# Chunk products by row halves in turn, one half's PSUM tile from another pool

## The chip, the cores and the metric

One NeuronCore of a Trainium2 chip runs the whole forward pass. TensorE (PE) multiplies into PSUM, VectorE (DVE), ScalarE (ACT) and GpSimd (POOL) work on tiles in SBUF and PSUM, and SyncE (SP) issues the DMAs. Each engine runs its instructions in the order in which they stand in its stream. The metric is the device time of one execution in microseconds, as the median of several runs; less is better.

## The reference, cut to what matters

Six layers and a final norm, on 256 tokens of width 2048. The first and the fourth are RWKV-7 mixers: five kinds of projections, and per head (32 heads of 64) a recurrence over tokens.

```
xx = shift(h) - h
r, k, v, g = [(h + xx * mu[j]) @ w_in[j] for j in range(4)]
...
def step(state, inp):                        # per head, S is 64 x 64
    r_t, w_t, k_t, v_t, a_t, b_t = inp
    sa = einsum('bhij,bhj->bhi', state, a_t)
    state = state * w_t + sa * b_t^T + v_t * k_t^T
    y_t = einsum('bhij,bhj->bhi', state, r_t)
...
y = group_norm(y) + bonus
return (y * silu(g)) @ w_out
```

The other layers are attention, pooling, an LRU with attention, and an mLSTM; the change does not touch their code.

## The kernel before

**Projections.** `proj` (line 239) makes one 256 x 512 output: 96 matmuls of line 262, three for each product, since an f32 operand is split into a high and a low part (`wh`, `wl`, `ah`, `al`; lines 220 and 221 split the weights on ACT and DVE). An RWKV layer has k, r and v (two groups of 512 columns each, then again two), then four gate projections, then the output projection, first with chunks 0 to 2 of its input, then with chunk 3. That is 1536 matmuls of line 262 up to the last gate.

**Blocks.** Beside the projections run eight head blocks (`rwkv_block`, four heads of 64 each, 256 columns). Tokens are cut into four chunks of 64, and a block goes through these steps:

- loads, small projections (line 724) and transposes (789), from which `AR` and `BK` come (DVE and POOL, 801 to 815); the bonus (828);
- the chunk products (842): for each half `f` of the block, four chunks `c` and two row halves `hp` of 64 rows, `BK` times `AR` into a PSUM tile for each `hp`, which DVE masks into `GM` (845). Each matmul leaves two records in the trace;
- the elimination: ACT copies (860) and 15 steps on DVE (871 to 881) that end in `Xc`, and from it `X` (932);
- `AV` (904), transposes `BT` (913), and the inversion: two products (929), two of blocks (956) with copies (958, 959) that complete `X`;
- four chunk rounds, each with PE products 990, 998, 1008 and 1022 and copies between them (the output goes to `yt`, 1026);
- group norm (1036 to 1049) and the gate: tile `z` (1055 or 1057). `acts_from` transposes `z` (line 277) and splits it for the output projection.

**PSUM pools.** In an RWKV layer there are four pools of two buffers: `ps` for projections, `gy` for the chunk rounds, `tp` and `gm` for the rest. `tp` serves lines 277, 724, 789, 828 and 842; `gm` serves 904, 913, 929 and 956.

```
BANKS = {True: {"ps": 2, "tp": 2, "gm": 2, "gy": 2}, False: {"ps": 4, "tp": 2, "gm": 2}}
```

Tiles of a pool are handed out in the order in which the program's text asks for them, each as soon as a buffer is free.

**Order.** The text is written by generators that are interleaved by an estimate of PE time (`spawn`, `pump`); blocks start a fixed period apart, and have a high priority (`urgent`). The final order on each engine is made by a scheduler, which orders instructions by priority and by its own timeline, under the data and buffer dependences. So a small edit can move instructions all through a layer.

Of the kernel before, what the change touches and what calls it, by code (L numbers as in the profile page):

```python
# [23 lines left out]
ORDER = mybir.DependencyInfo(mybir.DependencyClass.NoSync, mybir.DependencyReason.DATA)  # L24
# [90 lines left out]
class Builder:  # L115
# [562 lines left out]
    def rwkv_block(self, ia, b):  # L678

        nc, I, S = self.nc, self.I, self.S  # L680
# [89 lines left out]
        AR = self.t("q4", [128, 2, 4, 128], F32, 8)  # L770
        BK = self.t("q4", [128, 2, 4, 128], F32, 8)
# [54 lines left out]
        for t in range(2):  # L826
            for f in range(2):
                nc.tensor.matmul(qb[:, t * 4 + f * 2:t * 4 + f * 2 + 2], pr[:, f, t * 128:t * 128 + 128], rkc[:, f],
                                 start=True, stop=True)
# [5 lines left out]
        GM = self.t("GM", [128, 4, 4, 128], F32, 3)  # L835
        gmask = self.c("gmask")
        for f in range(2):
            qs = [self.p("tp", (128, 4, 128)) for _ in range(2)]
            for c in range(4):
                for hp in range(2):  # L840
                    rs = slice(hp * 64, hp * 64 + 64)
                    nc.tensor.matmul(qs[hp][:, c], BK[rs, f, c], AR[rs, f, c], start=True, stop=True)  # L842
            self.pe(0.9)
            for hp in range(2):
                nc.vector.tensor_tensor(GM[:, f * 2 + hp].rearrange("p (q a) n -> p q (a n)", a=2),  # L845
                                        qs[hp].rearrange("p (q a) n -> p q (a n)", a=2),
                                        gmask[:, f * 128:f * 128 + 256].unsqueeze(1).to_broadcast([128, 2, 256]), OP.mult)
            yield 1.0
# [7 lines left out]
        for i in range(4):  # L856
            rs = slice(i * 32, i * 32 + 32)
# [115 lines left out]
        rows = self.bcast(I["a_rows"][ia, b, 256:768], "rows", 512, 1)  # L973
# [3 lines left out]
        for c in range(4):  # L977
# [18 lines left out]
            for hp in range(2):  # L996
                for f in range(2):
                    nc.tensor.matmul(gy[ar[f], 4 + hp], X[ar[f], (f * 2 + hp) * 2 + pq], G[ar[f], f, hp],
                                     start=first, stop=True, skip_group_check=True)
# [5 lines left out]
            if c < 3:  # L1005
                for hh in range(4):
                    f, hp = hh // 2, hh % 2
                    nc.tensor.matmul(gy[half[hp], 6 + f], BT[:, f * 3 + c, half[hp]], UV[:, hh * 64:hh * 64 + 64],
                                     start=first, stop=True, skip_group_check=True)
# [10 lines left out]
            for hh in range(4):  # L1020
                f, hp = hh // 2, hh % 2
                nc.tensor.matmul(gy[kr[f], hh], GM[:, hh, c, to[f]:to[f] + 64], UV[:, hh * 64:hh * 64 + 64],
                                 start=first, stop=True, skip_group_check=True)
# [838 lines left out]
```

## Time and profile before

| | us |
|---|---|
| median of 3 runs | 3160.73 |
| lowest and highest | 3151.62, 3163.76 |
| the profiled execution | 3169.43 |
| its span | 3167.6 |
| PE busy | 3017.3 (95%) |
| DVE busy | 2247.9 (71%) |
| ACT busy | 1703.7 (54%) |

The span is the time from the first to the last instruction of the profiled execution. Busy time is the union of an engine's instructions; PE is the matmul side, weight loads count apart. A row of a timeline merges equal instructions that follow each other.

### The profile page before, as it was taken

The numbers are of one execution on the slowest core, as the hardware profiler recorded it, in microseconds if no ns is written. First come the engines' busy times: TensorE is split into PE (matmuls) and PEld (weight loads), VectorE is DVE, ScalarE is ACT, GpSimd is POOL, SyncE is SP. The second block draws the span as 40 slices with busy tenths as digits, with TensorE's granted clock in tenths as the row PEclk, the third lists the DMA queues.
The fourth block names the chain that finished last, engine by engine and source line by source line (L and its number), as shares of the span: only waits on it lengthen the run. The fifth ranks groups of instructions, "written<-read, shape, count | busy, mean of one in ns | idle before, by whom it ended". The sixth has DMA issues, their size and how long they took to land. (4 is left out here: it accounts for less than half of the span.)

```text
span 3167.6 us, 48383 instructions
## 1 busy us (share of the span) xinstructions
PE 3017.3 (95%) x17064; PEld 2448.3 (77%) x17064; DVE 2247.9 (71%) x4811; ACT 1703.7 (54%) x3320; POOL 483.3 (15%) x386
## 2 busy tenths in 40 slices
PE   6989999998999999999989899999999999999998
PEld 5777777777888888888867677777777788888886
DVE  7868778765667667676596787898557765756765
ACT  4555555545555555555545554545357755554554
POOL 1012223120112111010011132321201200000101
PEclk9999999998999999999999998999999999999999
DMA  7865564375556556667678555633765566665665
GB/s 235 321 209 169 176 212 148 127 232 184 178 170 179 176 173 215 192 215 214 207 263 280 200 189 175 199 121 121 246 186 157 170 186 193 182 204 169 189 185 169
DMA packets 327011, 610.77 MB, mean 193 GB/s; under 512 B 33856, under 2 KB 60776, under 8 KB 326768
## 3 DMA queue, kind: packets, MB, share of 16 engines
q1 hardware_dynamic: 326768, 607.68, 61.2%
q8 instruction: 134, 2.20, 0.3%
q14 instruction: 109, 0.89, 0.1%
HBM read 544.66 MB, written 62.93 MB: 192 GB/s over the span
## 5 line engine op out<-in xcount | busy, mean ns | idle before, releaser
L221 DVE TENSOR_TENSOR wl<-wr,wh 128x512 fp32r<-128x512 f32 x1728 | 1243.8, 731 | 713.2 <-ACT wh L220 687.3
L220 ACT CAST wh<-wr 128x512 fp32r<-128x512 f32 x1728 | 1055.6, 621 | 1078.3 <-PE qps L262 515.6
L262 PE MATMUL qps<-wl,ah 128*128 128x512 f32 x3424 | 1382.2, 404 | 7.3 <-DVE wl L221 7.2
L262 PE MATMUL qps<-wh,al 128*128 128x512 f32 x3424 | 1364.9, 399 | 2.0 <-DVE al L221 2.0
L262 PE MATMUL qps<-wh,ah 128*128 128x512 f32 x3424 | 1259.0, 404 | 46.1 <-ACT wh L220 11.8
L262 PEld LDWEIGHTS qps<-wh,ah 128*128 128x128 f32 x3424 | 655.1, 192 | 191.6 <-issue 20.4
L262 PEld LDWEIGHTS qps<-wl,ah 128*128 128x128 f32 x3424 | 657.6, 192 | 147.2 <-DVE wl L221 13.1
L262 PEld LDWEIGHTS qps<-wh,al 128*128 128x128 f32 x3424 | 656.0, 192 | 139.9 <-DVE al L221 4.5
L1107 POOL TENSOR_TENSOR q<-q,gain 128x1024 f32<-128x1024 f32 (+1 forms) x15 | 35.0, 2332 | 380.1 <-ACT sq L1101 380.1
L277 PE MATMUL qtp<-cst,q 128*128 128x128 f32 x388 | 62.4, 291 | 30.3 <-DVE q L436 9.7
L482 DVE SCALAR_TENSOR_TENSOR e<-q,vec,q 128x256 f32<-128x256 f32 x192 | 86.6, 504 | 0.0
L277 PEld LDWEIGHTS qtp<-cst,q 128*128 128x128 f32 x388 | 48.8, 149 | 43.7 <-issue 20.5
L842 PE MATMUL qtp<-q,q 64*128 64x128 f32 x512 | 76.3, 312 | 3.5 <-POOL q L815 3.3
L860 ACT COPY Md<-GM 32x128 f32<-32x128 f32 x128 | 54.8, 428 | 38.6 <-DVE GM L845 37.4
L842 PEld LDWEIGHTS qtp<-q,q 64*128 64x128 f32 x512 | 62.7, 209 | 14.6 <-issue 5.9
L1038 POOL TENSOR_TENSOR yt<-yt,gn_m 128x512 f32<-128x512 f32 x16 | 19.1, 1192 | 300.5 <-DVE gn_m L1037 191.6
L321 POOL TENSOR_TENSOR rstd<-rs_v,mhalf 128x2 f32<-128x2 f32 x7 | 5.0, 710 | 383.8 <-DVE rs_v L319 333.6
L304 POOL TENSOR_TENSOR rk_y<-ss,mhalf 128x8 f32<-128x8 f32 x16 | 28.1, 1756 | 217.7 <-DVE ss L715 117.3
L876 DVE TENSOR_TENSOR mb<-mb,Xc 128x120 f32<-128x120 f32 (+14 forms) x240 | 59.8, 249 | 0.4
L845 DVE TENSOR_TENSOR GM<-qtp,cst 128x512 f32<-128x512 f32 x64 | 43.0, 684 | 18.7 <-PE qtp L842 16.7
L871 DVE STREAM_SHUFFLE mb<-Mc 128x120 f32<-128x120 f32 (+14 forms) x240 | 50.6, 223 | 0.1
L881 DVE TENSOR_TENSOR Xc<-Xc,mb 128x112 f32<-128x112 f32 (+6 forms) x224 | 47.6, 213 | 0.1
(377 smaller groups left out, 3032.6 us busy)
## 6 DMA issues: line engine op xcount, KB each, us to landing
wr<-a_w_in SPq DMA_DIRECT2D x256, 512.0 KB
wr<-b_w_in SPq DMA_DIRECT2D x160, 512.0 KB
wr<-odd_w_in SPq DMA_DIRECT2D x128, 512.0 KB
wr<-even_w_in SPq DMA_DIRECT2D x72, 512.0 KB
wr<-a_w_out SPq DMA_DIRECT2D x64, 512.0 KB
wr<-c_w_in SPq DMA_DIRECT2D x64, 512.0 KB
ah<-mix SPq DMA_DIRECT2D x32, 512.0 KB
al<-mix SPq DMA_DIRECT2D x32, 512.0 KB
```

The source lines that it names most:

```text
L220: self.nc.scalar.copy(hi, src)
L221: (eng or self.nc.vector).tensor_tensor(lo, src, hi.bitcast(F32), OP.subtract)
L262: nc.tensor.matmul(o[:, cs], u[:, kk, sl], v[k][:, cs], start=st and x == 0 and c1 == 0, stop=sp and x == 2, skip_group_check=True)
L277: nc.tensor.transpose(q[:, f, t * 128:t * 128 + 128], src[:, t, (fp * 2 + f) * 128:(fp * 2 + f) * 128 + 128], self.ident)
L482: ins = nc.vector.scalar_tensor_tensor(m[:, f], st.xx[c][:, ft], mu, st.h[c][:, ft], OP.mult, OP.add)
L842: nc.tensor.matmul(qs[hp][:, c], BK[rs, f, c], AR[rs, f, c], start=True, stop=True)
L845: nc.vector.tensor_tensor(GM[:, f * 2 + hp].rearrange("p (q a) n -> p q (a n)", a=2), qs[hp].rearrange("p (q a) n -> p q (a n)", a=2), gma ...
L860: nc.scalar.copy(Md[rs, :, us].rearrange("p c u -> p u c"), GM2[rs, us, (1 - i // 2) ^ f, rs])
L871: nc.vector.stream_shuffle(mb[:, 0:15 - r], Mc[:, r + 1:16], [r] * 16 + [r + 16] * 16)
L876: nc.vector.tensor_tensor(mb[:, 0:n], mb[:, 0:n], Xc[:, r:r + 1].to_broadcast([128, n, 8]), OP.mult)
L881: nc.vector.tensor_tensor(Xc[:, r + 2:16], Xc[:, r + 2:16], mb[:, 1:n], OP.add)
L1107: nc.gpsimd.tensor_tensor(e3, e3, gain.unsqueeze(1).to_broadcast([128, 2 * nh, 128]), OP.mult)
```

## The change

For each half `f`, the tile of the second row half comes from `gm` in place of `tp`, and each matmul gets an ordering edge to the one before it, so that the scheduler must keep the order hp 0, hp 1, hp 0, and so on. The edge is one of order on PE and no semaphore.

```
-            qs = [self.p("tp", (128, 4, 128)) for _ in range(2)]
+            qs = [self.p("tp", (128, 4, 128)), self.gm((128, 4, 128))]
+            turn = None
             for c in range(4):
                 for hp in range(2):
                     rs = slice(hp * 64, hp * 64 + 64)
-                    nc.tensor.matmul(qs[hp][:, c], BK[rs, f, c], AR[rs, f, c], start=True, stop=True)
+                    mm = nc.tensor.matmul(qs[hp][:, c], BK[rs, f, c], AR[rs, f, c], start=True, stop=True)
+                    if turn is not None:
+                        self.tc.add_manual_dep(mm.ins, turn.ins.name, ORDER, reason="the halves of the rows take turns")
+                    turn = mm
```

Later lines of the file move down by four; line 842 becomes 843.

First place, the products of block 1 in the first layer, on PE. `qtp` and `qgm` are tiles of the pools `tp` and `gm`, `qps` of a projection; numbers tell tiles apart. Before, around the second row half of f = 0:

```order
L262 MATMUL qps_1514<-wh_1683,al_1253 128x512
L262 MATMUL qps_1513<-wh_1687,ah_1252 128x512
L842 MATMUL qtp_2543<-q4_2409,q4_2410 128x128 x4
L929 MATMUL qgm_2068<-Y_2066,GM_1804 64x64 x16
L842 MATMUL qtp_2560<-q4_2409,q4_2410 128x128 x4
L262 MATMUL qps_1513<-wl_1688,ah_1252 128x512
```

After, the first matmul of f = 0, and the rest of f = 0, which stands 77 projection matmuls further on, behind the last inversion product of block 0:

```order
L917 MATMUL qgm_2037<-cst_96,q4_1708 128x128 x3
L828 MATMUL qtp_2534<-rkc_2495,e2_2452 128x2 x4
L843 MATMUL qtp_2542<-q4_2409,q4_2410 128x128
L262 MATMUL qps_1513<-wl_1666,ah_1181 128x512
L262 MATMUL qps_1513<-wh_1665,al_1182 128x512
```

```order
L960 MATMUL qgm_2158<-X_2061,W_2132 32x32 x15
L843 MATMUL qgm_2543<-q4_2409,q4_2410 128x128
L843 MATMUL qtp_2542<-q4_2409,q4_2410 128x128
L843 MATMUL qgm_2543<-q4_2409,q4_2410 128x128
L843 MATMUL qtp_2542<-q4_2409,q4_2410 128x128
L843 MATMUL qgm_2543<-q4_2409,q4_2410 128x128
L843 MATMUL qtp_2542<-q4_2409,q4_2410 128x128
L843 MATMUL qgm_2543<-q4_2409,q4_2410 128x128
L262 MATMUL qps_1909<-wl_2045,ah_1697 128x512
```

The products of block 1 stood ahead of the inversion's second product before, and stand behind its fourth now. 28 of the 32 halves are cut in this way.

Second place, PE at the end of the gate projections of the first layer, from the last gate matmul on (`qps_6504`). Before, up to the first matmuls of the output projection (`qps_7052`):

```order
L262 MATMUL qps_6504<-wh_6978,al_4810 128x512
L1022 MATMUL qgy_6671<-uv_6672,GM_6068 64x64 x4
L1008 MATMUL qgy_7124<-uv_7125,q4_6911 64x64 x4
L277 MATMUL qtp_7093<-cst_96,z_5468 128x128 x2
L277 MATMUL qtp_7100<-cst_96,z_2572 128x128 x4
L1022 MATMUL qgy_7124<-uv_7125,GM_6714 64x64 x4
L990 MATMUL qgy_7168<-S_7154,q4_6581 128x128 x2
L262 MATMUL qps_7052<-wh_7136,ah_7073 128x512
```

After, the first rows and, further on, those at the first transposes of z:

```order
L262 MATMUL qps_6504<-wh_6978,al_4810 128x512
L1002 MATMUL qgy_5955<-G_5961,X_5656 64x64 x4
L843 MATMUL qtp_6740<-q4_6581,q4_6582 128x128
L933 MATMUL qgm_6306<-Y_6304,GM_6068 64x64 x16
L1012 MATMUL qgy_5955<-uv_5956,q4_5618 64x64 x4
L933 MATMUL qgm_6341<-X_6302,W_6323 64x64 x16
L1026 MATMUL qgy_5955<-uv_5956,GM_5437 64x64 x4
L994 MATMUL qgy_6025<-S_5865,q4_5308 128x128 x2
L960 MATMUL qgm_6380<-Y_6377,GM_6068 32x32 x16
L1002 MATMUL qgy_6025<-G_6031,X_5656 64x64 x4
L960 MATMUL qgm_6415<-X_6302,W_6379 32x32 x16
L843 MATMUL qgm_6716<-q4_6581,q4_6582 128x128
```

```order
L843 MATMUL qgm_6741<-q4_6581,q4_6582 128x128
L843 MATMUL qtp_6740<-q4_6581,q4_6582 128x128
L843 MATMUL qgm_6741<-q4_6581,q4_6582 128x128
L277 MATMUL qtp_7075<-cst_96,z_2572 128x128 x4
L908 MATMUL qgm_6915<-vt_6367,GM_6714 64x64
L1012 MATMUL qgy_6493<-uv_6494,q4_6264 64x64 x4
```

The inversion of block 6 and the products of block 7 stood beside gate matmuls before, and stand between the last gate matmul and the first output matmul now. In the second RWKV layer more stands there: from the inversion of block 5 on.

Third place, PE at the transposes of block 7's output (`qtp_7402`) in the first layer. Before, within the output projection of chunks 0 to 2 (`qps_7675`, `qps_7676`):

```order
L262 MATMUL qps_7676<-wl_7724,ah_7082 128x512
L262 MATMUL qps_7676<-wh_7723,al_7083 128x512
L277 MATMUL qtp_7402<-cst_96,z_6861 128x128 x4
L262 MATMUL qps_7675<-wh_7727,ah_7082 128x512
L262 MATMUL qps_7676<-wh_7727,ah_7082 128x512
```

After, within that of chunk 3 (`qps_7820`, `qps_7821`):

```order
L262 MATMUL qps_7821<-wl_7829,ah_7371 128x512
L262 MATMUL qps_7821<-wh_7828,al_7372 128x512
L1026 MATMUL qgy_7264<-uv_7265,GM_6714 64x64 x4
L277 MATMUL qtp_7402<-cst_96,z_6861 128x128 x4
L262 MATMUL qps_7820<-wh_7846,ah_7371 128x512
```

The transposes stood 54 projection matmuls earlier, and stand directly behind block 7's last chunk product now.

## Rows read from the trace of the kernel before

**Rows 1.** The page, busy time, share and count of each engine:
```profile
PE 3017.3 (95%) x17064; PEld 2448.3 (77%) x17064; DVE 2247.9 (71%) x4811; ACT 1703.7 (54%) x3320; POOL 483.3 (15%) x386
```

**Rows 2.** Windows, blocks' stretches: length, busy by engine, clock, DMA share, GB/s:
```profile
157.05:629.31 472.26, 449.24 (x3642) 355.62 (x3640) 366.47 (x1164) 254.27 (x564) 111.53 (x97) 0.95 0.54 176
1740.49:2208.62 468.13, 437.12 (x3583) 345.50 (x3581) 381.25 (x1174) 246.16 (x549) 115.06 (x97) 0.93 0.52 170
```

**Rows 3.** PE's waits, 157 to 629 us: total us, times, longest:
```profile
PE qgm L913 <- ACT q L915: 4.0, 2, 3.4
```

**Rows 4.** Timeline of PE around the first output matmul: start, us, what:
```profile
626.16 0.39 PE L262 MATMUL qps<-wh,al 128*128 128x512 f32 x1
...
629.31 0.50 PE L262 MATMUL qps<-wh,ah 128*128 128x512 f32 x1
...
2206.70 0.50 PE L262 MATMUL qps<-wh,al 128*128 128x512 f32 x1
...
2208.62 0.50 PE L262 MATMUL qps<-wh,ah 128*128 128x512 f32 x1
```

**Rows 5.** Groups by form, the chunk products: busy us, mean ns, idle before:
```profile
L842 PE MATMUL qtp<-q,q 64*128 64x128 f32 x512 | 76.3, 312 | 3.5 <-POOL q L815 3.3 <-ACT bon L832 0.2
```

**Rows 6.** Timeline of PE, two halves of block 0:
```profile
155.96 1.16 PE L842 MATMUL qtp<-q,q 64*128 64x128 f32 x16
...
161.36 1.71 PE L842 MATMUL qtp<-q,q 64*128 64x128 f32 x16
```

**Rows 7.** Timeline of PE, bursts of one row half, and a lone matmul:
```profile
208.08 1.16 PE L842 MATMUL qtp<-q,q 64*128 64x128 f32 x8
...
521.96 2.07 PE L842 MATMUL qtp<-q,q 64*128 64x128 f32 x8
...
491.92 0.48 PE L842 MATMUL qtp<-q,q 64*128 64x128 f32 x2
```

**Rows 8.** Windows of line 262 alone, first stretch:
```profile
157.05:629.31 472.26, 299.70 (x1132) 215.85 (x1132) 0.95 0.54 176
```

**Rows 9.** Timeline of DVE, block 7 of the first layer: mask, X, last copy:
```profile
554.45 0.69 DVE L845 TENSOR_TENSOR GM<-qtp,cst 128x512 f32<-128x512 f32 x1
...
578.03 1.12 DVE L932 TENSOR_TENSOR X<-Xc,cst 128x512 f32<-128x512 f32 x1
...
605.65 0.42 DVE L959 COPY X<-qgm 32x256 f32<-32x256 f32 x1 [0.24 <-ACT X L958]
```

**Rows 10.** Timeline of DVE: block 0, a chunk round and a mask of the second layer:
```profile
162.56 1.29 DVE L845 TENSOR_TENSOR GM<-qtp,cst 128x512 f32<-128x512 f32 x2 [2.08 <-PE qtp L842]
...
235.74 0.42 DVE L959 COPY X<-qgm 32x256 f32<-32x256 f32 x1
...
1853.11 0.29 DVE L1026 COPY yt<-qgy 64x128 f32<-64x128 f32 x1 [1.13 <-ACT yt L1026]
...
1861.04 0.28 DVE L1026 COPY yt<-qgy 64x128 f32<-64x128 f32 x1
...
2094.02 0.69 DVE L845 TENSOR_TENSOR GM<-qtp,cst 128x512 f32<-128x512 f32 x1 [0.64 <-PE qtp L842]
...
2113.46 1.12 DVE L932 TENSOR_TENSOR X<-Xc,cst 128x512 f32<-128x512 f32 x1
```

**Rows 11.** Timeline, block 7 of the first layer: chunk copies, z, transposes:
```profile
631.82 0.29 DVE L1026 COPY yt<-qgy 64x128 f32<-64x128 f32 x1
...
647.70 0.28 DVE L1026 COPY yt<-qgy 64x128 f32<-64x128 f32 x1
...
677.16 0.28 DVE L1026 COPY yt<-qgy 64x128 f32<-64x128 f32 x1
...
692.19 0.69 DVE L1055 SCALAR_TENSOR_TENSOR z<-yt,z 128x512 f32<-128x512 f32 x1 [1.19 <-POOL yt L1049]
...
696.86 0.60 PE L277 MATMUL qtp<-cst,z 128*128 128x128 f32 x4
```

**Rows 12.** Windows, a stretch with waits in it:
```profile
200.00:250.00 50.00, 44.97 (x353) 36.54 (x354) 35.12 (x123) 23.73 (x50) 10.19 (x10) 0.86 0.57 192
```

## Prediction

> **What bounds the kernel now.** I read the engines' busy shares first: TensorE (PE) is busy 95% of the span [rows 1], nearly all of it with the projections of line 262. So the time changes in two ways only: through PE's own work, and through time in which PE's in-order stream has nothing to run. The change touches the two RWKV layers alone. I cut out of each the stretch in which the eight head blocks run beside the projections [rows 2]: PE is busy 449.2 of 472.3 us and 437.1 of 468.1 us. That leaves 54 us idle in all, in short waits such as the 4.0 us of [rows 3]. The block chain is thus almost wholly hidden, and the question is whether it stays so.
>
> At the end of the gate projections little waits: from the last gate matmul to the first of the output projection PE needs 3.15 us in the first layer (626.16 to 629.31) and 1.9 us in the second [rows 4].
>
> **The chunk products themselves.** The 256 matmuls leave 512 records and 76.3 us of PE [rows 5], 2.38 us for each of 32 halves f (two layers, eight blocks, two halves). The row halves of PE overlap where they alternate: 16 records that do took 1.16 us, 16 that mostly don't 1.71 us [rows 6]. A burst of one row half takes 1.16 us for 8 records, so 2.3 us for both; at a low clock it took 2.07 us [rows 7]. In the order of instructions 7 of the 32 halves alternate wholly before.
>
> After the change 4 of 32 stand in one piece, at 1.16 us. The other 28 are cut as the first place of the order shows: one matmul alone, and 7 alternating much later. A lone matmul takes 0.48 us [rows 7], the seven 7/8 of 1.16, together 1.5 us. That is 4 x 1.16 + 28 x 1.5 = 47 us, 30 us less than 76. Some of the 76 us is low clock, which would strike other instructions instead, so I take **-25 us**, with 0 (the overlap is lost) and -35 as ends. The Trainium skill (TensorEngine Tiling (Array Packing), "Theoretical Speedup") gives up to 2x for a contraction of at most 64 rows; by it the term would be -38 us. The rows with their cut halves give less, and they decide.
>
> **What the second pool costs.** The `gm` tile of a half is asked for after all `gm` tiles of the block before, down to the last of its inversion. The order shows the result: the first product of block 1 goes out early into `tp`, and its `gm` partner stands behind the last inversion product (line 956, 960 after) of block 0. Before, nothing tied them. So the blocks now form one ring: products, mask, elimination, X, four inversion products, next block's products. Meanwhile both `tp` buffers are held by half-made tiles, and what asks for `tp` later waits too, above all the transposes of the gated output (line 277, tile z) that the output projection needs. That is the new wait; I cost it by place.
>
> *Inside a layer* it is covered. Between two blocks' products the order has 167 to 183 projection matmuls in the first four rings of the first layer, at 299.7 us / 1132 = 0.265 us each [rows 8], and some 172 other matmuls of two records. All other PE work of the stretch is (449.2 - 299.7) us over 3642 - 1132 records [rows 2, 8], 60 ns a record. A ring so has 44 + 21 = 65 us of PE work to hide in. The ring itself took 51.6 us in block 7 (554.45 to 606.07) [rows 9] and 73.6 us in block 0 (162.56 to 236.16) [rows 10], both beside a second chain. I take 0, with -15 and +40 as ends.
>
> *End of the gates, first layer.* After the change 150 matmuls stand between the last gate and the first output matmul (20 before): the inversion of block 6, then the products of block 7, then the transposes. 150 x 2 x 60 ns = 18 us is work that merely moved. The gap is longer: from X to the last copy block 7 took 28 us (578.03 to 606.07) [rows 9] between projections, while the vector steps in it sum to some 4 us. Without projections in between I take 14 us, 2.5 us for the products, and 8 us, a fast chunk round (1853.11 to 1861.04) [rows 10], for the round, transposes and split behind them: 24.5 us, **+6 us** over the moved work (0 to 25).
>
> *End of the gates, second layer.* The order has 315 matmuls there (16 before): the inversion of block 5, the products of block 6, its elimination and inversion, the products of block 7. A whole ring is bare. 14 + 2.5 us; then the longer of two chains, mask to X (2094.02 to 2114.58, 20.6 us) [rows 10] and three chunk rounds of block 5 (8 us fast; 15.9 us from 631.82 to 647.70 [rows 11]), for which I take 27 us; then 14 + 2.5 + 8 us: 68 us. 315 x 2 x 60 ns = 38 us of it moved here. **+30 us** (8 to 70).
>
> *End of block 7, both layers.* The blocks end later, and at the third place of the order the last chunk product (line 1022, 1026 after) stands directly ahead of the transposes of block 7's output, behind which only matmuls that need them are left. Before, this had cover: last chunk copy at 677.16, z ready at 692.88, transposes at 696.86 [rows 11], PE running all along. After, it is bare: 15.7 us, and some 1.5 us until the split tiles are there, 17 us a layer: **+34 us** (26 to 42).
>
> *Clock.* The stretch from 200 to 250 us, with short waits in it, ran at a mean granted clock of 0.86 [rows 12] and so lost 7 us of its 50. I take 2 us for each of four long new waits: **+8 us** (0 to 15). The Trainium skill (TensorE: Matmul & The Clock Gate, "HAM oscillation") says that idle gaps put PE back to half rate; the row fits that without proving it.
>
> Vector, scalar and pool work stay the same: the mask reads a PSUM tile of the same size from either pool. Loads keep their bytes; some of later blocks move behind weight loads in SP's queue, and a DMA share of 0.54 and 0.52 [rows 2] leaves room for that, so 0.
>
> Sum: -25 + 0 + 6 + 30 + 34 + 8 = **+53 us**. The profiled execution took 3169.4 us (span 3167.6), 8.7 us above the median of 3160.7; it would become 3222, and against the median **3214 us**, 1.7% slower. A measurement of this kernel tells no less than about 0.5%, 16 us, from no change.
>
> **Rivals.** (a) *Not slower: one ring instead of two chains takes out the idle time inside the layers.* Some of those 54 us [rows 2] come from chains that meet in PE's order, as the wait of the transposes of line 913 for scalar copies [rows 3]. If 37 us or more of the 54 go, the change is within 0.5%; all gone gives 3160. Against it: most are waits inside one chain, and these stay. To be faster by 16 us the bare places must take their short ends besides. 9% within, 3% faster.
> (b) *The ring is longer than its cover.* If it needs 5 us more than its 65 us in each of 14 rings, 70 us come on top: 3284. The 73.6 us of block 0 speaks for it; against it, two chains then shared the vector engine, and one does now. 14%.
> (c) *The products gain nothing*, since pairs into different pools don't overlap or the lone matmul costs more: -25 falls away, 3239. The alternating rows [rows 6] speak against it. 6%.
> My forecast holds 68%.
>
> **Range.** 3168 to 3275: down into the within-0.5% case, up to most of (b); the wide ends of the three bare places make it no narrower. Faster 3%, within 0.5% 9%, slower 88%.
>
> **What will show it.** Products of line 843 (842 before) near 47 us busy. In both layers the mask and scalar copies of a block come only after the inversion's last copies (line 963 after) of the block before. Between the last gate matmul and the output projection a gap of about 25 us in the first layer and 68 us in the second, and some 17 us with PE idle ahead of block 7's transposes in both. If the gaps are 18 and 38 us with PE busy throughout, those terms are mis-sized; if PE idles inside the layers far beyond 54 us, (b) holds; if the blocks' rings still overlap, I have misread the pool.

## The result, and the profile after

The changed kernel takes 3196.15 us (median of 4 runs, 3192.70 to 3199.95), the one before beside it 3162.06: a ratio of 1.0116, 95% interval [1.0098, 1.0133], slower by 1.2%. The profiled executions differ by 29.7 us in span (3197.3, 3167.6). Single executions of one kernel spread: among those of the one before that were run beside run 8 the shortest took 3147.36 us at a granted clock of 0.978 and the longest 3171.49 us at 0.971, so a term of a few us in the balances below is within the scatter.

The page of the changed kernel, to set against [rows 1]: PE is busy 6 us less, and the span is 30 us longer.

```profile
PE 3010.9 (94%) x17064; PEld 2431.1 (76%) x17064; DVE 2239.1 (70%) x4811; ACT 1703.3 (53%) x3320; POOL 476.8 (15%) x386
```

Windows of the chunk products alone, line 843, whole span (length, PE busy, weight loads, clock, DMA share, GB/s). They take 55.9 us where they took 76.3 [rows 5]:

```profile
0.00:3197.30 3197.30, 55.88 (x512) 43.86 (x512) 0.97 0.61 191
```

Where the blocks now meet is seen on DVE at the end of block 0, in the timeline after. Both masks of block 1 (line 849) come only after the last copy of block 0's inversion (line 963), as the one ring has it. The same order holds for every later block in both layers: four masks, then the inversion's last copy, then the next four masks.

```profile
226.89 0.42 DVE L963 COPY X<-qgm 32x256 f32<-32x256 f32 x1 [0.95 <-ACT X L962]
...
228.78 0.69 DVE L849 TENSOR_TENSOR GM<-qtp,cst 128x512 f32<-128x512 f32 x1
229.39 0.68 DVE L849 TENSOR_TENSOR GM<-qgm,cst 128x512 f32<-128x512 f32 x1
```

The windows after, by stage (columns as in [rows 2]). First the blocks' stretch up to the last gate matmul and the gap from there to the first output matmul, in the first and in the second layer:

```profile
162.06:586.01 423.95, 403.19 (x3113) 315.81 (x3112) 333.26 (x1027) 233.24 (x509) 99.80 (x89) 0.97 0.58 190
586.01:614.89 28.88, 23.64 (x284) 19.28 (x282) 21.25 (x53) 14.31 (x39) 9.34 (x8) 0.65 0.15 49
...
1751.34:2150.60 399.26, 375.56 (x2753) 292.66 (x2753) 308.47 (x921) 214.82 (x459) 91.67 (x77) 0.97 0.59 193
2150.60:2218.70 68.10, 53.52 (x595) 42.81 (x594) 48.65 (x172) 29.17 (x78) 20.00 (x18) 0.62 0.13 38
```

The gaps are 28.9 and 68.1 us long (3.15 and 1.9 before [rows 4]), and PE is busy for 82% and 79% of them, at a granted clock of 0.65 and 0.62: it works on the blocks' small products, and no projection runs.

For a balance I cut each layer at the same projection matmuls in both kernels: from block 0's first products to the matmul that stands ahead of block 7's transposes after the change, the wait there, and the rest of the output projection. (Before, these transposes stand 54 projection matmuls ahead of that cut, so there is no wait at it.) Before:

```profile
157.05:710.88 553.83, 526.61 (x4029) 416.97 (x4028) 420.37 (x1252) 289.93 (x630) 129.87 (x109) 0.96 0.56 182
...
711.11:744.72 33.61, 26.19 (x118) 20.77 (x116) 21.01 (x41) 19.84 (x46) 0.71 (x1) 0.87 0.72 230
1740.49:2296.29 555.80, 517.57 (x3983) 409.00 (x3981) 435.63 (x1265) 283.24 (x619) 133.95 (x109) 0.94 0.55 179
...
2296.51:2328.67 32.16, 25.50 (x117) 20.21 (x116) 21.00 (x41) 19.76 (x46) 0.71 (x1) 0.92 0.73 228
```

After:

```profile
162.06:710.30 548.24, 516.88 (x4002) 404.72 (x4000) 416.56 (x1242) 287.11 (x626) 120.80 (x104) 0.96 0.56 183
710.30:725.18 14.88, 1.89 (x14) 1.04 (x13) 4.72 (x10) 2.50 (x5) 6.48 (x5) 0.65 0.41 129
725.18:754.51 29.33, 25.38 (x117) 19.83 (x117) 20.05 (x38) 18.59 (x44) 0.71 (x1) 0.95 0.63 197
1751.34:2313.69 562.35, 519.17 (x3954) 405.08 (x3953) 419.84 (x1257) 283.26 (x617) 123.09 (x103) 0.93 0.53 173
2313.69:2329.25 15.56, 1.89 (x14) 1.04 (x13) 4.79 (x10) 2.51 (x5) 6.48 (x5) 0.67 0.70 221
2329.25:2358.63 29.38, 25.53 (x116) 19.91 (x117) 20.04 (x38) 18.56 (x44) 0.71 (x1) 0.94 0.65 201
```

The first parts change by -5.6 and +6.6 us, the gaps inside them included. Ahead of block 7's transposes there are now 14.9 and 15.6 us (0.2 before), and the rest is 4.3 and 2.8 us shorter. A layer so costs +4.8 and +19.1 us; the remaining 5.8 of the 29.7 us lie outside these stretches.

The bare wait itself in the timeline after. It is the chain of block 7's group norm and gate, where before it ran beside projections [rows 11]:

```profile
710.61 0.46 PE L1026 MATMUL qgy<-uv,GM 128*64 128x64 f32 x8
...
712.10 0.28 DVE L1030 COPY yt<-qgy 64x128 f32<-64x128 f32 x1
...
722.64 0.69 DVE L1059 SCALAR_TENSOR_TENSOR z<-yt,z 128x512 f32<-128x512 f32 x1 [4.11 <-POOL yt L1053]
...
723.39 1.12 PE L277 MATMUL qtp<-cst,z 128*128 128x128 f32 x4 [12.32 <-DVE z L1059]
```

### The profile page after: what moved, and what is told of

Its sections match the earlier page's. It is cut to its first block, busy times and chain, and to the rows that moved or that the text cites. A ratio compares the mean times of both kernels' runs of the same rounds, so it can differ in the third digit from the quotient of the medians.

```text
span 3197.3 us, 48385 instructions
## 1 busy us (share of the span) xinstructions
PE 3010.9 (94%) x17064; PEld 2431.1 (76%) x17064; DVE 2239.1 (70%) x4811; ACT 1703.3 (53%) x3320; POOL 476.8 (15%) x386
## 5 line engine op out<-in xcount | busy, mean ns | idle before, releaser
L262 PEld LDWEIGHTS qps<-wl,ah 128*128 128x128 f32 x3424 | 652.8, 191 | 147.1 <-DVE wl L221 15.6
L277 PEld LDWEIGHTS qtp<-cst,q 128*128 128x128 f32 x388 | 48.1, 147 | 43.3 <-issue 18.5
L801 POOL TENSOR_TENSOR q<-e,e 128x256 f32<-128x256 f32 x32 | 27.8, 889 | 222.5 <-DVE e L799 189.7
L277 PE MATMUL qtp<-cst,z 128*128 128x128 f32 x160 | 28.4, 298 | 27.2 <-DVE z L1059 25.3
L843 PE MATMUL qtp<-q,q 64*128 64x128 f32 x256 | 48.3, 317 | 3.0 <-POOL q L815 3.0
L875 DVE STREAM_SHUFFLE mb<-Mc 128x120 f32<-128x120 f32 (+14 forms) x240 | 50.6, 222 | 0.0
```

What stands on the lines that cost most here:

```text
L262: nc.tensor.matmul(o[:, cs], u[:, kk, sl], v[k][:, cs], start=st and x == 0 and c1 == 0, stop=sp and x == 2, skip_group_check=True)
L277: nc.tensor.transpose(q[:, f, t * 128:t * 128 + 128], src[:, t, (fp * 2 + f) * 128:(fp * 2 + f) * 128 + 128], self.ident)
L843: mm = nc.tensor.matmul(qs[hp][:, c], BK[rs, f, c], AR[rs, f, c], start=True, stop=True)
L875: nc.vector.stream_shuffle(mb[:, 0:15 - r], Mc[:, r + 1:16], [r] * 16 + [r + 16] * 16)
```

## The experiments

Each ratio is to the kernel before, run on the same chip in the same job. The first four were made on the theory that the ring through `gm` is the price, and that it is paid at the layers' ends.

**Run 1, turns without the second pool.**

```
-            qs = [self.p("tp", (128, 4, 128)), self.gm((128, 4, 128))]
+            qs = [self.p("tp", (128, 4, 128)) for _ in range(2)]
```

> Both tiles from tp as before, the ordering edges kept. My theory (the ring through the gm pool costs, the taking of turns gains): no bare places, products near 45 us of PE in place of 76, time 3140 us (3125 to 3160), faster than before. Rival (the edges themselves hold the products of a block back, the pool is harmless): slower than before, 3180 us or more.

Measured: 3180.91 us, 1.0065 [1.0048, 1.0081]. The products took 52.6 us and PE's busy time fell by 20 us, to 2996.8, but the span grew to 3179.3: the saved time came back as idle time. The rival's number came. Turns alone cost time.

**Run 2, the second pool without the turns.**

```
-                    if turn is not None:
-                        self.tc.add_manual_dep(mm.ins, turn.ins.name, ORDER, reason="the halves of the rows take turns")
```

> Second tile from gm, no ordering edges. My theory: the ring stays for the second row half and the products alternate less, so slower than before, 3165 to 3195 us, with the bare wait of some 13 us ahead of block 7's transposes again. Rival (the edges do the harm): 3162 us, as before.

Measured: 3191.73 us, 1.0105 [1.0084, 1.0125]. That is inside the theory's range, and the bare waits ahead of block 7's transposes stand (18.8 and 20.5 us). The pool alone costs nearly as much as the whole change, and so the two costs don't add.

**Run 3, the pools swapped.**

```
-            qs = [self.p("tp", (128, 4, 128)), self.gm((128, 4, 128))]
+            qs = [self.gm((128, 4, 128)), self.p("tp", (128, 4, 128))]
```

> Changed kernel with the pools swapped: the first matmul of a half waits for gm, so no half is cut and no tp buffer is held by a half-made tile. My theory (the ring costs): the bare places stay, 3175 to 3195 us, a little under the changed kernel by the uncut halves (28 x 0.3 = 8 us). Rival (the tp buffers held meanwhile cost): back to 3165 us or less.

Measured: 3203.75 us, 1.0142 [1.0121, 1.0163]. That is above the theory's range. No half waits half made any more, and the products take 40.4 us, the least of all runs; it is the slowest kernel all the same, with 34.3 and 58.4 us at the ends of the gates and 14.9 us ahead of block 7's transposes in both layers. That the held `tp` tiles are the price falls with it.

**Run 4, the last three blocks with both tiles from `tp`.**

```
-            qs = [self.p("tp", (128, 4, 128)), self.gm((128, 4, 128))]
+            qs = [self.p("tp", (128, 4, 128)), self.gm((128, 4, 128)) if b < 5 else self.p("tp", (128, 4, 128))]
```

> Changed kernel, but blocks 5 to 7 of each layer take both tiles from tp. My theory (the cost lies in the bare places at the layers' ends alone, inside a layer the ring is covered): the gaps of 29 and 68 us behind the last gate matmul shrink to 5 us or less, and time falls to 3145 us (3130 to 3165). Rival (the ring also costs inside the layers): 3175 us or more, for five of eight blocks keep it.

Measured: 3189.10 us, 1.0092 [1.0073, 1.0112]. The gaps at the gates' ends fell to 5.3 and 6.7 us, as wanted, and the time hardly followed: the rival's number came, and the bare waits are still there, 16.0 us in each layer. That the gaps in themselves are the price falls too. The next runs cut by blocks, and by what the edges hold.

**Run 5, both tiles from `tp`, and the edges hold one row half after the other.**

```
-            for c in range(4):
-                for hp in range(2):
+            for hp in range(2):
+                for c in range(4):
```

> Edges and tiles as in the run with both tiles from the first pool, but the order that the edges hold is all four products of one row half, then all four of the other: nothing alternates, while both tiles must still be free before the second half starts. The price of alternation alone is the difference to that run. My theory (PE time saved by alternation is real, some 20 us, but the edges that hold a half together delay the blocks and turn it into idle time): the products of line 843 near 74 us busy, block 7 no later than before (its products stand at projection matmuls 1267 to 1308, before 1248 to 1320), idle time near that of before, 3160 to 3170 us. Rival (holding a half together costs some 35 us by itself, whatever the order): 3190 to 3205 us. Rival (the lone order matters for nothing, 3181 as with turns).

Measured: 3144.55 us, 0.9951 [0.9939, 0.9964], below the range expected. The products are back at 72.5 us, and the kernel is 36 us faster than with turns (run 1) and 0.5% faster than before. Windows of the whole span, run 1 and then run 5 (columns as in [rows 2]):

```profile
0.00:3179.30 3179.30, 2996.79 (x17064) 2419.94 (x17064) 2265.83 (x4811) 1704.74 (x3322) 473.01 (x386) 0.97 0.61 192
```

```profile
0.00:3144.00 3144.00, 2999.41 (x17064) 2433.37 (x17064) 2245.75 (x4811) 1703.83 (x3320) 475.85 (x386) 0.98 0.61 194
```

PE is equally busy; run 1 has 182.5 us without PE work, run 5 has 144.6 (before 150.4). A first half that takes turns needs its second tile from its second matmul on; in one piece it goes ahead as soon as its own tile is free. In the order block 7's products end at projection matmul 1384 with turns and 1308 without.

**Runs 6 to 8, by blocks.** Run 6: turns with both tiles from `tp`, in blocks 0 to 4 alone. Run 7: the change in blocks 0 to 4, blocks 5 to 7 as before. Run 8: the reverse of run 7.

```
 run 6   qs = [self.p("tp", (128, 4, 128)) for _ in range(2)]
         if turn is not None and b < 5:
 run 7   qs = [self.p("tp", (128, 4, 128)), self.gm((128, 4, 128)) if b < 5 else self.p("tp", (128, 4, 128))]
         if turn is not None and b < 5:
 run 8   the same two lines with b > 4
```

> Both tiles from the first pool; blocks 0 to 4 alternate by edges, blocks 5 to 7 have no edges, as before. Block 7's products stand at projection matmuls 1304 to 1344 (with edges everywhere 1330 to 1384). My theory (what costs is the late end of the last block's chain): the wait ahead of block 7's transposes in the second layer goes, some 12 us of PE are saved, idle time in the layers stays at some 70 us; 3160 to 3170 us. Rival (waits inside the layers, from chains that meet in PE's order, cost the most): 3175 to 3185 us, as with edges everywhere.

> Blocks 0 to 4 as in the change (second tile from the small pool, edges), blocks 5 to 7 as before. The order has 22 and 20 matmuls at the two ends of the gates (before 20 and 16, the change 150 and 315) and block 7's products at 1418 to 1460. My theory (the ring of the first five blocks moves the whole chain back, and the bare wait ahead of block 7's transposes is what remains of it): the gaps at the end of the gates near 4 us, the bare waits shorter than the change's 15 us a layer, some 5 to 10 us; 3170 to 3180 us. Rival (the ring itself costs inside the layers, the ends nothing): 3185 to 3200 us, as with the last blocks changed in other ways.

> Blocks 5 to 7 as in the change (second tile from the small pool, edges), blocks 0 to 4 as before. The reverse of the run with the change in blocks 0 to 4 alone (3158 us). The order has 15 matmuls at each end of the gates and 12 between the last chunk product and block 7's transposes. My theory now (what costs is what happens to the last three blocks, whatever goes ahead of them): 3180 to 3195 us, with a bare wait of 14 to 18 us ahead of block 7's transposes in both layers. Rival (the price needs the whole ring from block 0 on, and the two halves of it are each free): 3155 to 3170 us.

Measured: run 6 3164.09 us, 1.0017 [1.0004, 1.0030]; run 7 3158.16, 0.9990 [0.9979, 1.0001]; run 8 3188.76, 1.0092 [1.0075, 1.0110]. Run 6 lies in its theory's range, though PE idles for 84 us in its two first parts (65 before). In the time the ring of the first five blocks is free; the change in the last three alone carries most of the price. Run 7 lies below both its ranges, though its bare waits did not shrink to 5 to 10 us as my theory had it. The windows of run 7, cut as above:

```profile
159.64:697.59 537.95, 512.28 (x3993) 401.72 (x3992) 422.47 (x1240) 287.86 (x625) 123.42 (x104) 0.97 0.57 187
697.59:713.64 16.05, 2.35 (x23) 1.35 (x21) 5.01 (x11) 2.68 (x6) 6.48 (x5) 0.69 0.30 104
713.64:742.99 29.35, 25.62 (x116) 19.99 (x117) 20.04 (x38) 18.61 (x44) 0.71 (x1) 0.94 0.63 197
1733.81:2271.16 537.35, 507.09 (x3986) 397.38 (x3984) 425.18 (x1258) 283.25 (x618) 126.25 (x104) 0.97 0.55 182
2271.16:2286.05 14.89, 1.89 (x15) 1.04 (x13) 4.72 (x10) 2.51 (x5) 6.49 (x5) 0.70 0.67 209
2286.05:2315.77 29.72, 26.28 (x116) 20.74 (x117) 20.51 (x40) 18.60 (x44) 0.71 (x1) 0.90 0.63 198
```

The first parts are 15.9 and 18.5 us shorter than before, and pay for the bare waits of 16.1 and 14.9 us. In run 4 the same parts, with the last three blocks taking turns, give most of that back; its windows:

```profile
160.63:713.33 552.70, 512.58 (x3994) 401.59 (x3992) 424.58 (x1240) 287.20 (x625) 119.17 (x104) 0.96 0.56 181
...
1749.23:2302.98 553.75, 515.78 (x3977) 402.71 (x3976) 426.77 (x1259) 282.94 (x617) 126.78 (x106) 0.94 0.54 177
```

552.7 and 553.8 us against 538.0 and 537.4: 31 us, of which PE's busy time is 9 and idle time 22. PE's waits in the first layer's part tell which (total us, times, longest), run 4 and then run 7:

```profile
PE qgm L933 <- DVE Y L942: 5.8, 3, 3.8
PE qgy L1026 <- DVE S L1022: 5.3, 3, 2.9
PE qgy L1026 <- DVE S L1020: 5.1, 2, 3.1
```

```profile
PE qgy L1026 <- DVE S L1020: 3.2, 1, 3.2
...
PE qgy L1026 <- DVE S L1022: 1.0, 2, 0.5
```

The first of these waits does not occur in run 7's part. The long gap of the change has become short waits of the inversion and of the chunk rounds: the wait has moved, and not gone. That holds for the first layer, with 14 of the 22 us. In the second layer the largest difference is another: PE waits 14.1 us for loads at the small projections (line 724), where run 7 waits 7.9.

**Run 9, the change with one row half after the other.** The loops over `c` and `hp` swapped as in run 5, the tiles as in the change.

```
-            for c in range(4):
-                for hp in range(2):
+            for hp in range(2):
+                for c in range(4):
```

> The change with its order turned off: first half into tp, second half into gm, and the edges hold all four products of the first row half ahead of all four of the second, in all blocks. A first half so no longer keeps a tp tile half made while it waits for gm: in the order block 2's first product (projection matmul 592) stands ahead of block 1's last (606), and the gates' ends hold 12 and 19 matmuls (the change 150 and 315). Theory 1 (it is the alternation across two pools, which holds a tp tile until gm comes, that costs): near the pool alone or better, 3160 to 3180 us. Theory 2 (the order of the gm requests alone delays the blocks, as the run with the pool and no edges suggests): 3185 to 3200 us, with a bare wait of some 15 to 20 us ahead of block 7's transposes.

Measured: 3187.44 us, 1.0077 [1.0058, 1.0096]. Theory 2: with the ring loosened and nothing alternating, the requests to `gm` still cost 25 us, and the bare waits stand (14.9 and 17.5 us). Together with the runs before, this tells the pool from the order. The second pool takes the ratio from 1 to 1.0105 without edges (run 2), from 1.0065 to 1.0116 with turns (run 1, the change), and from 0.9951 to 1.0077 with one half after the other (runs 5 and 9): it costs 0.5% to 1.3% in each order. Turns in place of one half after the other cost 1.1% with one pool and 0.4% with two.

**Runs 10 and 11, one row half after the other in the last three blocks,** with blocks 0 to 4 as in run 7 (run 10) and as in run 6 (run 11). Both replace the two loops; tiles of blocks 0 to 4 as there, the others from `tp`.

```
+            for i in range(8):
+                for hp, c in [(i % 2, i // 2) if b < 5 else (i // 4, i % 4)]:
```

> Blocks 0 to 4 as in the change; blocks 5 to 7 with both tiles from the first pool and the edges that hold one row half after the other. If the last three blocks set the price and this order is good for them: 3140 to 3155 us, the bare wait ahead of block 7's transposes at 10 to 16 us. If the 0.5% that the run with one half after the other won was luck of the order: as with blocks 5 to 7 of before, 3155 to 3165 us.

> Both tiles from the first pool; blocks 0 to 4 take turns by edges, blocks 5 to 7 have one row half after the other. Theory (the turns save some 12 us of PE in the first five blocks, the other order keeps the last three early): 3135 to 3150 us, below both kernels. Rival (turns in the first five blocks lose in waits inside the layers what they save, as the run without edges in the last three had it): 3155 to 3170 us.

Measured: 3167.42 us, 1.0018 [1.0005, 1.0030], and 3156.60 us, 0.9984 [0.9967, 1.0001]. Against runs 7 and 6 the same edit is worth, by the ratios, +9 and -10 us. So an edit to the order of three blocks moves this kernel by some 10 us either way without a reason that I could name; run 10 lies above both its ranges, run 11 in its rival's.

**Run 12, the change in blocks 0 to 3 alone.** As run 7 with `b < 4`.

```
             qs = [self.p("tp", (128, 4, 128)), self.gm((128, 4, 128)) if b < 4 else self.p("tp", (128, 4, 128))]
             if turn is not None and b < 4:
```

> Blocks 0 to 3 as in the change, blocks 4 to 7 as before: one block fewer than in the run at 3158 us. In the order block 7's products stand at projection matmuls 1344 to 1392 (there 1418 to 1460), and nothing of the last chunk round stands bare ahead of block 7's transposes in either layer. Theory (each bare wait there costs the kernel 11 to 12 us: some 15 us long, 3 to 4 us given back behind it): 3158 us less 23 us, and 2 to 4 us more for the block that no longer alternates: 3132 to 3145 us. Rival (a bare wait only collects work that must be done anyhow): 3155 to 3165 us.

Measured: 3143.20 us, 0.9951 [0.9934, 0.9968], inside the theory's range, and with run 5 the fastest. But my expectation was wrong in one point: the bare wait went in the first layer only. Windows of run 12:

```profile
157.97:703.71 545.74, 515.46 (x4014) 406.36 (x4013) 428.43 (x1251) 289.44 (x629) 127.88 (x109) 0.97 0.57 185
703.71:703.94 0.23, 0.23 (x3) 0.18 (x1) 0.00 (x0) 0.04 (x1) 0.00 (x0) 1.00 1.00 383
703.94:732.51 28.57, 24.22 (x118) 19.01 (x116) 21.02 (x41) 19.94 (x46) 0.71 (x1) 0.98 0.80 253
1723.83:2255.78 531.95, 505.23 (x3985) 397.12 (x3984) 422.85 (x1260) 283.40 (x618) 129.67 (x106) 0.97 0.56 184
2255.78:2270.67 14.89, 1.89 (x14) 1.04 (x13) 4.72 (x10) 2.51 (x5) 6.49 (x5) 0.66 0.67 211
```

In the first layer the wait (16.1 us in run 7) is gone, the part ahead of it is 7.8 us longer, the rest 0.8 shorter: in this one comparison, in which block 4's products change as well, a bare wait of 16 us is worth 9. In the second layer the wait stays and the part ahead is 5.4 us shorter, so not all of the 12 us between runs 7 and 12 (by the ratios) is the wait's.

**All runs by where block 7's products end** (its last product, counted in projection matmuls from the start, in the order of instructions, in both layers; the last gate matmul is number 1536 in the first layer and 6816 in the second):

| kernel | ends at | products, us | ratio |
|---|---|---|---|
| run 5 | 1308, 6624 | 72.5 | 0.9951 |
| before | 1320, 6624 | 76.3 | 1 |
| run 11 | 1330, 6662 | 59.7 | 0.9984 |
| run 6 | 1344, 6660 | 60.1 | 1.0017 |
| run 1 | 1384, 6699 | 52.6 | 1.0065 |
| run 12 | 1392, 6750 | 63.4 | 0.9951 |
| run 7 | 1460, 6770 | 60.4 | 0.9990 |
| run 10 | 1460, 6779 | 61.7 | 1.0018 |
| run 9 | 1494, 6816 | 71.7 | 1.0077 |
| run 8 | 1513, 6793 | 67.5 | 1.0092 |
| run 4 | 1516, 6796 | 50.6 | 1.0092 |
| run 2 | 1536, 6831 | 70.7 | 1.0105 |
| the change | 1536, 6816 | 55.9 | 1.0116 |
| run 3 | 1536, 6816 | 40.4 | 1.0142 |

Every kernel whose last block comes later than 1460 is slower by 0.8% to 1.4%, whatever its products take; up to 1460 all but run 1 lie within 0.5% of the one before. The edits of these kernels differ in more than the end of block 7, so the table shows that the two go together, and not that the late end is the cause.

## Why the prediction was right, and where its sizes were off

The changed kernel shows the mechanism that was forecast: the products take less, the blocks form one ring, and the layers' ends, bare of projections, cost more than the products give. The time is 18 us below the forecast, inside its range; in the profiled executions the sum was to be +53 us and is +30. By its steps:

- **Products, -25.** They fell by 20.4 us, to 55.9 and not to 47, so rival (c) fell. Some 4 of these 9 us are the clock: 80 of the 512 records ran in the two gaps at the clock's lower level (the last section has rows of them) and take 12.5 us, where at the 0.10 us of each of the others they would take 8. I had counted all bursts at the full clock. Where all 32 halves take turns, 31 of them in one piece (run 3), the products take 40.4 us of 76.3, a factor of 1.9. The "up to 2x" of the Trainium skill (TensorEngine Tiling (Array Packing), "Theoretical Speedup") agrees with that run. As a gain in time the term did not stand by itself: the turns alone took 20 us off PE's busy time and made the kernel slower (run 1). In the order before, six halves alternated wholly and not seven; nothing rests on it.
- **Inside the layers, 0.** Better than that. In run 7, which has the ring without the late end, the two first parts lose 34 us together, of which its products account for 16 (76.3 to 60.4); 25 of the 34 us are PE's busy time and 9.5 idle time. Some 4 us of the busy time have only moved into the bare waits (2.35 and 1.89 us there, 0.2 before), and the granted clock rose from 0.96 and 0.94 to 0.97. Rival (a), which wanted 37 us of idle time to go, was thus there for 9.5. Rival (b), rings longer than their cover, fell: up to the last gate matmul the change leaves PE 20.8 and 23.7 us idle in stretches of 424 and 399 us.
- **Ends of the gates, +36, and clock, +8.** The lengths, 28.9 and 68.1 us, are close to those forecast (24.5 and 68), but that was partly luck. The working filled them with 18 and 38 us of moved work and 36 us of waits; the windows show 23.6 and 53.5 us of work, 83 and 90 ns a record where 60 were reckoned, and 20 us of waits. Work at a granted clock of 0.65 and 0.62 stood in for waits that did not come, and +8 for the clock was too little: PE's busy time fell by 6 us while the products fell by 20, so all other work took some 14 us more. Against run 7 the change's first parts are 10.3 and 25.0 us longer: 35 us, 17 of busy and 18.6 of idle time, where 44 were forecast with the clock. Runs 2, 4 and 8, whose gaps are 4 to 7 us, gain no more than 8 us on the change, so it isn't the gap as such that is paid for. My reading is that the last blocks' lateness costs, as a gap or as many short waits.
- **Bare wait ahead of block 7's transposes, +34.** 14.9 and 15.6 us long, near the 17 forecast, but worth less: what stands behind it is 7 us shorter, which leaves 23. The step took the length of a wait for its price. Run 12 gives 9 us for such a wait of 16.
- **Elsewhere, nothing.** 5.8 us, most of it ahead of block 0's first products (157.05 to 162.06); run 5 shows 4.1 us there (161.11) and takes less time, so I count it as scatter.

By these, -34 and +35 and +23 and +6 make +30; the products' 20 us are inside the first two.

That the second pool costs in each order is shown by the three pairs of runs under run 9, and that the change in the last three blocks carries most of the price by runs 7 and 8. That it costs through their lateness rests on the table and is not shown by a run that moves the end of block 7 alone. Why PE's order then has the chains' matmuls so close behind what they wait for, in run 4 above all, was read from its waits and not tested by a run; and the 9 and 10 us by which runs 10 and 11 move in opposite senses stay open. So does the 0.5% of run 5, which removes no work and alternates nothing. Its second layer's first part, to set against the 555.80 us before:

```profile
1741.02:2280.23 539.21, 504.97 (x3981) 399.32 (x3981) 429.83 (x1265) 284.18 (x619) 131.69 (x108) 0.97 0.56 184
```

It is 16.6 us shorter, 12.6 of them PE's busy time and 4 idle time, at a granted clock of 0.97 for 0.94. All six executions of run 5 had a mean granted clock of 0.977 to 0.981, those of the kernel before beside it 0.971 to 0.976. The gain thus goes with the clock; whether the new order brought it is not shown.

## What to carry to other kernels

Taking turns between row halves saves PE time (up to 36 of 76 us here, run 3), but it needs both PSUM tiles at once; where that holds up a chain that must end before the work covering it runs out, the saving can come back as idle time, as it did here in run 1. Make such an edit first in the blocks that have cover left (here 0 to 3) and look at where the last one ends. And price a forecast wait by what becomes shorter behind it, not by its length alone.

## What the hardware showed that was not expected

Matmuls of the two row halves start almost together. In the timeline after, two pairs at full clock, 226.61 and 226.72, are 0.11 us apart, and within a pair the records start at most 0.01 us apart:

```profile
226.61 0.27 PE L843 MATMUL qgm<-q,q 64*128 64x128 f32 x1
226.61 0.27 PE L843 MATMUL qtp<-q,q 64*128 64x128 f32 x1
226.72 0.27 PE L843 MATMUL qgm<-q,q 64*128 64x128 f32 x1
226.72 0.27 PE L843 MATMUL qtp<-q,q 64*128 64x128 f32 x1
...
605.15 0.42 PE L843 MATMUL qgm<-q,q 64*128 64x128 f32 x1
605.16 0.42 PE L843 MATMUL qtp<-q,q 64*128 64x128 f32 x1
605.37 0.42 PE L843 MATMUL qgm<-q,q 64*128 64x128 f32 x1
605.37 0.42 PE L843 MATMUL qtp<-q,q 64*128 64x128 f32 x1
```

In the gap at the end of the gates (605.15 on) the step is 0.21 to 0.22 us: the lower of the two levels of the clock, 1.2 GHz. Windows of this gap, cut where the granted clock changed (columns as in [rows 2]):

```profile
586.01:591.79 5.78, 2.40 (x44) 1.62 (x42) 4.95 (x9) 3.44 (x8) 1.22 (x1) 1.00 0.36 109
591.79:612.27 20.48, 18.62 (x220) 15.51 (x220) 13.72 (x37) 9.16 (x26) 5.59 (x5) 0.50 0.08 25
612.27:614.89 2.62, 2.62 (x22) 2.16 (x21) 2.58 (x10) 1.71 (x6) 2.53 (x2) 1.00 0.29 100
```

Behind the last gate matmul PE was idle for 3.4 of 5.8 us, and then its clock fell to the lower level. There it stayed for 20.5 us, in which PE was busy for 18.6 us with the blocks' small products and with none of the projection's; it rose 2.6 us ahead of the first output matmul. The Trainium skill (TensorE: Matmul & The Clock Gate, "HAM oscillation") tells of waits that put the clock back. The fall agrees with it; that the clock then stayed low through 18.6 us of work is not explained by waits.
